# Two of the four sums of the up weights made by adding transfers, values handled in pairs, and eight groups of up tiles by seven products

## The chip, the cores and the metric

One core of one Trainium2 chip runs the whole program in one launch. The metric is the device time of one execution in microseconds (us), the median over several runs. The engines named here are PE (TensorE matmuls; its weight loads are PEld), DVE (VectorE), ACT (ScalarE), POOL (GpSimd), SP (SyncE, which issues most transfers), and 16 DMA engines that move the data.

## The reference, cut to what matters

The block takes 256 tokens, puts 16 learned meta tokens in front, and runs one layer: RMSNorm, one input projection, two kinds of attention (8 heads each), an output projection with residual, then a gated MLP. All data are float32. The change touches the MLP and, in time, what runs beside the attention:

```python
def conv_glu(x, w_gate, w_up, conv_w, conv_b, w_down):   # x (1, 272, 2048); D_FF = 5632
    g = x @ w_gate
    u = x @ w_up
    gp = jnp.pad(g, ((0, 0), (pad, pad), (0, 0)))
    gc = conv_b
    for i in range(CONV_W):                              # CONV_W = 3
        gc = gc + conv_w[i] * gp[:, i:i + L]
    return (jax.nn.silu(gc) * u) @ w_down
```

## The kernel before

Every float32 matmul is made of three matmuls on fp32r halves: a number is split into a rounded part ("hi", by ACT) and a rest ("lo", by DVE), and hi·hi, hi·lo and lo·hi are added in PSUM (`mm3`, lines 606 to 608). So each weight passes ACT once (`whi<-raw`, line 238) and DVE once (`wlo<-raw,whi`, line 242). Weights come in pieces of 128 rows by up to 1024 columns into five buffers `raw` (one more, `more_raw`, in the MLP); the halves have four buffers each (`whi`, `wlo`). A buffer `raw` is free for the next load when the lo split has read it.

The hidden width 5632 is 44 tiles of 128 features. `gate` and `up` are worked in pairs of tiles. Plainly, a pair takes four pieces of 1024 columns, and a piece is eight blocks of three matmuls. Six groups of four up tiles (`QUADS`, the group starts at tile 4, 10, 16, 22, 28, 36) are worked differently: the product of the tokens with four tiles is split in quarters for each pair of 128-row blocks, and seven products of quarters replace eight ("scheme"). For each of the eight row pairs of a group the weights' four quarters come as one piece of 1024 columns (`w_up_s`), and four sums of quarters have to be made from them: `weight_sums` does it with three subtractions on DVE, one 512 columns wide (two sums at once) and two of 256. The seven weight operands (three quarters, four sums) are split like any weights, in two pieces of 768 and 1024 columns. The sums of the tokens' quarters, S, are kept in `near` (a part of the later value buffer) or read again from DRAM (`s_up`). At a group's end `quad_out` combines the seven products on DVE and turns them with eight 128x128 transposes on PE (line 284). `w_down` has the same scheme for half of its columns, with its sums made on DVE as well.

A gate pair goes through `gated` (scale, a three-tap convolution on ACT and DVE, SiLU); `tile_up` or `quad_value` multiplies it with up; `finish_value` splits the value into `act` and, with both tiles of a pair there, `value_sums` forms the sums for `w_down_s` and `save_sums` stores them in DRAM (`s_down`). Tiles on this way sit in twelve buffers `mt` of 258 columns.

The order of everything is set when the program is built. `Flow` runs the generators with a cost for each instruction, and takes whichever can start first; what comes out is one fixed list for each engine. On the chip each engine works its list from the front, and a wait at the front holds all behind it. SP's list holds the loads (`load_weights`, `load_piece`). POOL's list holds, in the attention, the small copies `qs` and `p` (`meta_copies`, made before a softmax row is transposed on PE), the residual sums `res`, and `kr`, the sum of squares (`sum_h`) from which `scale_h` makes the factor `s_2` that the first gate and up tiles wait for. `work` is the list of MLP pieces: around each group's 16 scheme pieces the pieces of gate and up pairs are spread.

## Time and profile before

| what | value |
|---|---|
| median of 3 runs (lowest to highest) | 1108.91 us (1108.28 to 1108.98) |
| the profiled execution: its own time / its span | 1108.62 us / 1106.7 us |
| PE, DVE, ACT, POOL busy | 99%, 90%, 66%, 13% of the span |
| moved by DMA | 239.41 MB, mean 216 GB/s |
| granted TensorE clock | full over the whole span |

The profile was taken from one execution on the chip. Its page and its views give, for stretches or for groups of instructions, the time that an engine was busy, the mean time of one instruction, and what ended an engine's idle time. The roughly 2 us between the span and the execution's time lie outside the program's instructions. In time order PE works on the attention (to about 280 us), the output projection (280 to 376, with the last heads' rest beside it), gate and up with the groups (to 871), and down (to the end).

### The profile page before, as it was taken

The page shows a single profiled execution, that of the slowest core. Times are in us where ns is not written, and L with a number is a line of the kernel's source. Part 1 is how long each engine was busy: PE and PEld are TensorE (multiplying, and loading weights), DVE is VectorE, ACT ScalarE, POOL GpSimd, SP SyncE. Part 2 cuts the span into 40 slices and gives each one's busy share as a digit, 9 for nine tenths or more (in the row PEclk, how much of TensorE's full clock was granted, in tenths as well). Part 3 has the DMA queues.
Part 4 walks back from the last instruction along what each step waited for, and adds up shares of the span by engine and source line. Part 5 has one row for each costly group of instructions (what it writes and reads, how often), then busy time and mean ns, then how long its engine had stood idle before and what let it go on. Part 6 is the DMA issues. An engine that isn't in the chain of part 4 may idle for free.

```text
span 1106.7 us, 22544 instructions
## 1 busy us (share of the span) xinstructions
PE 1100.6 (99%) x8414; PEld 1061.8 (96%) x8414; DVE 990.8 (90%) x1837; ACT 735.1 (66%) x1470; POOL 140.0 (13%) x202
## 2 busy tenths in 40 slices
PE   9999999999999999999999999999999999999998
PEld 9999999999999999999999999999999988888888
DVE  8979888888878989999999999988988999999984
ACT  8788979798647776656666565665565565655663
POOL 3211222121433400000000000000000011100114
PEclk9999999999999999999999999999999999999999
DMA  9553434444665796657667577777688787777772
GB/s 323 199 172 124 148 127 151 139 163 134 230 188 161 207 343 229 198 181 243 224 193 230 179 248 241 238 229 244 203 275 299 260 299 250 251 258 266 281 249 77
DMA packets 72374, 239.41 MB, mean 216 GB/s; under 512 B 8136, under 2 KB 12744, under 8 KB 72264
## 3 DMA queue, kind: packets, MB, share of 16 engines
q1 hardware_dynamic: 71976, 237.69, 63.8%
q8 instruction: 66, 1.08, 0.4%
q14 instruction: 44, 0.36, 0.1%
q10 hardware_dynamic: 288, 0.27, 0.1%
HBM read 219.44 MB, written 17.83 MB: 214 GB/s over the span
## 4 chain that ended last, share of the span: by engine, by line
PE 90%; ACT 4%; DVE 3%; issue 1%; DMA 1%; POOL 0%; DVEq 0%; POOLq 0%; ACTq 0%
PE bank L278 24%; PE bank L606 18%; PE bank L607 18%; PE bank L608 18%; PE bank L1870 6%; PE bank L1871 3%; PE bank L284 2%; ACT whi L238 1%; ACT scr L238 1%; DVE wlo L242 1%; DVE scr L250 1%; DMA raw<-in_w_cq 1%; ACT qraw L238 0%; ACT bank L238 0%; DVE cols L258 0%
## 5 line engine op out<-in xcount | busy, mean ns | idle before, releaser
L238 ACT ACTIVATE whi<-raw 128x512 fp32r<-128x512 f32 (+2 forms) x479 | 358.1, 764 | 173.2 <-PE bank L607 83.5
L242 DVE TENSOR_TENSOR wlo<-raw,whi 128x512 fp32r<-128x512 f32 (+2 forms) x479 | 414.9, 885 | 43.2 <-ACT whi L238 42.1
L606 PE MATMUL bank<-hl,whi 128*128 128x258 f32 (+2 forms) x1528 | 438.5, 287 | 0.1
L607 PE MATMUL bank<-hl,whi 128*128 128x258 f32 (+2 forms) x1528 | 433.7, 284 | 0.0
L608 PE MATMUL bank<-hl,wlo 128*128 128x258 f32 (+2 forms) x1528 | 433.0, 283 | 0.2 <-DVE wlo L242 0.2
L608 PEld LDWEIGHTS bank<-hl,wlo 128*128 128x128 f32 x1528 | 290.1, 190 | 0.9 <-DVE wlo L242 0.7
L607 PEld LDWEIGHTS bank<-hl,whi 128*128 128x128 f32 x1528 | 289.6, 190 | 0.1
L606 PEld LDWEIGHTS bank<-hl,whi 128*128 128x128 f32 x1528 | 288.6, 189 | 0.5 <-ACT scr L238 0.3
L238 ACT ACTIVATE whi<-quarters 128x1024 fp32r<-128x1024 f32 x88 | 81.5, 950 | 64.8 <-PE bank L1870 46.0
L278 PE MATMUL bank<-whi,act 128*128 128x256 f32 (+1 forms) x420 | 111.5, 317 | 0.0
L1870 PE MATMUL bank<-act,whi 128*128 128x512 f32 x308 | 110.1, 397 | 0.0
L242 DVE TENSOR_TENSOR wlo<-quarters,whi 128x1024 fp32r<-128x1024 f32 x88 | 99.4, 1156 | 10.8 <-ACT whi L238 10.2
L266 POOL TENSOR_TENSOR mt<-mt,mt 128x256 f32<-128x256 f32 x7 | 6.8, 979 | 652.4 <-ACT mt L238 652.4
L1871 PE MATMUL bank<-act,wlo 128*128 128x256 f32 x308 | 86.4, 281 | 0.0
L278 PE MATMUL bank<-whi,sin 128*128 128x512 f32 (+1 forms) x272 | 83.5, 355 | 0.0
L278 PEld LDWEIGHTS bank<-whi,act 128*128 128x128 f32 x420 | 74.1, 189 | 5.7
L1870 PEld LDWEIGHTS bank<-act,whi 128*128 128x128 f32 x308 | 57.8, 188 | 13.9
L278 PE MATMUL bank<-whi,hl 128*128 128x256 f32 x288 | 66.5, 280 | 0.0
L278 PE MATMUL bank<-wlo,act 128*128 128x256 f32 (+1 forms) x210 | 66.3, 315 | 0.0
L238 ACT ACTIVATE whi<-more_raw 128x1024 fp32r<-128x1024 f32 (+2 forms) x46 | 44.1, 962 | 24.4 <-PE bank L607 9.9
L1871 PEld LDWEIGHTS bank<-act,wlo 128*128 128x128 f32 x308 | 58.1, 189 | 1.6
L278 PEld LDWEIGHTS bank<-whi,sin 128*128 128x128 f32 x272 | 49.5, 188 | 7.7
(278 smaller groups left out, 1947.9 us busy)
## 6 DMA issues: line engine op xcount, KB each, us to landing
raw<-in_w_gate SPq DMA_DIRECT2D x83, 512.0 KB, 5.0
raw<-in_w_in SPq DMA_DIRECT2D x52, 512.0 KB, 3.9
raw<-in_w_up_s SPq DMA_DIRECT2D x44, 512.0 KB, 4.9
quarters<-in_w_down_s SPq DMA_DIRECT2D x44, 512.0 KB, 6.9
raw<-in_w_up SPq DMA_DIRECT2D x34, 512.0 KB, 5.5
raw<-in_w_out SPq DMA_DIRECT2D x32, 512.0 KB, 4.0
raw<-in_w_down SPq DMA_DIRECT2D x32, 512.0 KB, 5.2
s_down<-sums SPq DMA_DIRECT2D x22, 512.0 KB, 4.1
```

The lines of the kernel that those rows point to most:

```text
L238: nc.scalar.activation(out, in_, f, **kw)
L242: nc.vector.tensor_tensor(out, a, b, op)
L250: nc.vector.scalar_tensor_tensor(out, a, s, b, op0, op1)
L266: nc.gpsimd.tensor_tensor(out, a, b, op)
L278: nc.tensor.matmul(o, l, r, start=start, stop=stop)
L284: nc.tensor.transpose(o, i, ident[:n, :n])
L606: nc.tensor.matmul(ps, whi, xhi, start=start, stop=False)
L607: nc.tensor.matmul(ps, whi, xlo, start=False, stop=False)
L608: nc.tensor.matmul(ps, wlo, xhi, start=False, stop=stop)
L1870: nc.tensor.matmul(ps, whi, x, start=start, stop=False)
L1871: nc.tensor.matmul(ps[:, :n], wlo, x[:, 0, :], start=False, stop=stop)
```

## The change

Four things are changed together.

1. **Sums by transfers.** A new thread `weight_sums_T` (started with the others, running once the tokens' squares are summed, some 34 us into the program) goes over the eight groups and, in steps of two row pairs, issues a transfer from DRAM to DRAM on SP (256 rows of 512 columns, 512 KB, into `t_up`) and, after it has landed, a second one on POOL's queue that adds the neighbouring columns to it (`accum_op=ALU.add`). That gives two of the four sums, with changed signs. 32 copies and 32 adding transfers are issued. In the MLP `load_pair` then loads each row pair's two sums (128x512, 256 KB) into the buffer where DVE used to make them, and `weight_sums` does only the two additions of 256 columns. The signs in `weight_sums`, `value_sums`, `quad_out` and `scheme_out` follow; the down part keeps its three instructions.
2. **Eight groups.** `QUADS` has eight starts in place of six, so eight up tiles that were worked plainly now go through seven products. Around each group stand three pairs of plain gate or up tiles (12 pieces); before there were four or six (16 or 24 pieces). The row pairs of a group are taken in the order `PAIRS`.
3. **Pairs.** Both tiles of a pair share one buffer `two` of 512 columns (four of them; of `mt` two are left). Splits, gate products of a group and value sums run on 512 or 256 columns at once in place of 256 and 128.
4. **Loads of S.** `load_S` for up is issued from `load_piece` two pieces ahead, in a thread of its own.

```diff
-QUADS = (4,10,16,22,28,36)
+QUADS = (4, 8, 14, 18, 24, 28, 34, 38)
+PAIRS = (0, 5, 1, 6, 2, 7, 3, 4)
+AHEAD_S = 2
...
+    TG = 2
+    sums_T = [
+        [(dpool.tile([TG, P, 512], F32, name=f"t_up{w}_{j}"), Event()) for j in range(KC // 2 // TG)]
+        for w in range(len(QUADS))
+    ]
+
+    def weight_sums_T():
+        yield ev_sum_x
+        for w, parts in enumerate(sums_T):
+            for j, (t, ev) in enumerate(parts):
+                src = io["w_up_s"][w][j * TG : (j + 1) * TG]
+                fl.cur.eng = None
+                yield "sp", 0
+                nc.sync.dma_start(t, src[:, :, :512])
+                fl.cur.t += 9000.0
+                yield "pool", 0
+                nc.gpsimd.dma_start(t, src[:, :, 256:768], accum_op=ALU.add)
+                fl.set(ev, 10000.0)
+                fl.cur.t += 2000.0
...
-        g, end = f // 2, (*QUADS, FC)[w + 1] // 2
-        rest = tile_pair("gate", g) + tile_pair("gate", g + 1)
-        for i in range(g + 2, end):
-            rest += tile_pair("gate", i) + tile_pair("up", i)
+        g = f // 2
+        rest = tile_pair(*(("up", g + 2) if w % 2 else ("gate", g + 4)))
+        rest = tile_pair("gate", g) + rest + tile_pair("gate", g + 1)
...
         if r.of == "down":
-            yield from load_S()
+            yield from load_S(r)
+        else:
+            (t, ev), i = r.T
+            yield ev
+            yield "sp", 600
+            load(r.sums[:, : 2 * r.q], t[i], r.ev_T, nc.sync)
...
         if r.of == "down":
             r.sums = yield from one(sums4)
-        t, raw, q = r.sums, r.raw, r.q
-        yield from TT(t[:, : 2 * q], raw[:, q : 3 * q], raw[:, : 2 * q], ALU.subtract)
+            yield from TT(r.sums[:, : 2 * q], r.raw[:, : 2 * q], r.raw[:, q : 3 * q], ALU.add)
+        else:
+            yield r.ev_T
+        t, raw = r.sums, r.raw
         fl.set(r.summed[0])
-        yield from TT(t[:, 2 * q : 3 * q], raw[:, 2 * q : 3 * q], t[:, :q], ALU.subtract)
-        yield from TT(t[:, 3 * q :], t[:, 2 * q : 3 * q], raw[:, 3 * q :], ALU.subtract)
+        yield from TT(t[:, 2 * q : 3 * q], t[:, q : 2 * q], raw[:, :q], ALU.add)
+        yield from TT(t[:, 3 * q :], t[:, 2 * q : 3 * q], raw[:, 3 * q :], ALU.add)
...
-        mts = Slots(tiles(mpool, 12, [P, NT], "mt"))
+        mts = Slots(tiles(mpool, 2, [P, NT], "mt"))
+        twos = Slots(tiles(mpool, 4, [P, 2 * SEQ], "two"))
...
-        yield from TT(A22, A21, A22, ALU.add)
-        yield from TT(A21, A11, A21, ALU.subtract)
-        yield from TT(A11, A22, A11, ALU.subtract)
-        yield from TT(A12, A12, A11, ALU.subtract)
+        yield from TT(b[:, 0:2], repeated(b[:, 1], 2), b[:, 0:4:3], ALU.subtract)
+        yield from TT(b[:, 3], b[:, 0], b[:, 3], ALU.subtract)
+        yield from TT(b[:, 2], b[:, 2], b[:, 3], ALU.add)
...
+    def quad_values(i, pt):
+        for c in range(2):
+            yield ev_gate[2 * i + c]
+        yield from TT(pairs[i], pt, pairs[i], ALU.mult)
+        fl.put(acc, pt)
+        yield from finish_values(i)
...
+    fl.spawn(weight_sums_T(), 3)
```

Three places show how the engines' lists change. First POOL in the attention, at the first pair of heads (`qs` are the gathered query columns, `p` the softmax rows). Before:

```order
L1326 COPY qs_187<-mqr_243 128x2x2 x2
L266 TENSOR_TENSOR p_163<-p_163 128x16
L266 TENSOR_TENSOR p_164<-p_164 128x16
L266 TENSOR_TENSOR p_165<-p_165 128x16
L266 TENSOR_TENSOR p_163<-p_163 128x16 x2
L266 TENSOR_TENSOR p_164<-p_164 4x16
```

and with the change:

```order
L327 DMA t_up_3_85<-in_w_up_s 256x512
L1363 COPY qs_219<-mqr_275 128x2x2 x2
L269 TENSOR_TENSOR p_195<-p_195 128x16
L269 TENSOR_TENSOR p_196<-p_196 128x16
L327 DMA t_up_0_86<-in_w_up_s 256x512
L269 TENSOR_TENSOR p_197<-p_197 128x16
L269 TENSOR_TENSOR p_195<-p_195 128x16 x2
L269 TENSOR_TENSOR p_196<-p_196 4x16
L327 DMA t_up_1_87<-in_w_up_s 256x512
```

Adding transfers now stand between the copies; each waits there for its copy of 512 KB to have landed. Of the 32, 21 stand ahead of the last `p` copy of the attention.

Second POOL at the change from the output projection to the MLP, where `kr` gathers the sum for `s_2`. Before:

```order
L266 TENSOR_TENSOR kr<-kr,scr_157 128x258
L266 TENSOR_TENSOR kr<-kr,scr_158 128x258
L266 TENSOR_TENSOR kr<-kr,scr_159 128x258
L266 TENSOR_TENSOR kr<-kr,scr_162 128x258
L266 TENSOR_TENSOR kr<-kr,scr_160 128x258
L266 TENSOR_TENSOR kr<-kr,scr_161 128x258
```

and with the change:

```order
L327 DMA t_up_3_109<-in_w_up_s 256x512
L269 TENSOR_TENSOR kr<-kr,scr_190 128x258
L269 TENSOR_TENSOR kr<-kr,scr_191 128x258
L269 TENSOR_TENSOR kr<-kr,scr_194 128x258
L269 TENSOR_TENSOR kr<-kr,scr_192 128x258
L327 DMA t_up_0_110<-in_w_up_s 256x512
L269 TENSOR_TENSOR kr<-kr,scr_193 128x258
```

Three adding transfers (one is five rows further up) stand among the fifteen additions, the last of them four additions before the end.

Third DVE in the first group of up tiles (`raw` and `more_raw` hold weights and their sums). Before:

```order
L242 TENSOR_TENSOR more_raw_5379<-raw_82 128x512
L242 TENSOR_TENSOR more_raw_5379<-raw_82,more_raw_5379 128x256
L242 TENSOR_TENSOR more_raw_5379<-more_raw_5379,raw_82 128x256
L242 TENSOR_TENSOR wlo_92<-raw_81,whi_88 128x1024
L242 TENSOR_TENSOR wlo_89<-raw_82,whi_85 128x512
L242 TENSOR_TENSOR wlo_89<-raw_82,whi_85 128x256
L242 TENSOR_TENSOR wlo_90<-raw_84,whi_86 128x1024
```

and with the change:

```order
L245 TENSOR_TENSOR raw_117<-raw_117,more_raw_5454 128x256 x2
L245 TENSOR_TENSOR wlo_125<-raw_115,whi_121 128x1024
L245 TENSOR_TENSOR wlo_126<-raw_118,whi_122 128x1024
L245 TENSOR_TENSOR wlo_123<-more_raw_5454,whi_119 128x512
L245 TENSOR_TENSOR wlo_123<-more_raw_5454,whi_119 128x256
L245 TENSOR_TENSOR wlo_124<-raw_116,whi_120 128x1024
```

The sum of 512 columns is gone from each row pair; the two of 256 and the splits of 512, 256 and 1024 columns stay.

More of the change, by code (lines that the diff above doesn't have):

```diff
@@ L47 @@
 ST = SF // P
[L48 removed]
+QUADS = (4, 8, 14, 18, 24, 28, 34, 38)
+PAIRS = (0, 5, 1, 6, 2, 7, 3, 4)
+AHEAD_S = 2
 def near_to(g):
[L53 removed]
+    return sum(f <= FC - KC + 2 * g for f in QUADS)
 AHEAD, BEHIND = 3, 8
@@ L494, in load_piece @@
         p = pieces[n_loads[0]]
+        for u in pieces[n_loads[0] + AHEAD_S : n_loads[0] + AHEAD_S + 1]:
+            if isinstance(u, Quarters) and u is u.pair.pieces[0] and u.pair.of == "up":
+                fl.spawn(load_S(u.pair))
         n_loads[0] += 1
@@ L502, in load_piece, with load_S @@
         load(p.raw[:, : p.n], p.src, p.loaded, nc.sync)
+    def load_S(r):
+        if r.near:
+            r.ev_S = ev_near[r.g]
+            return
+        r.S = yield from one(s_parts)
+        src, saved = saved_sums[r.of][r.g]
+        yield saved
+        yield "sp", 600
+        load(r.S, src, r.ev_S, nc.sync)
     def load_pair(r):
@@ L635, in hl_free @@
         fl.put(quarters if i < 2 else sums4, t)
-    dpool = ctx.enter_context(tc.tile_pool(name="dpool", bufs=1, space=bass.MemoryType.DRAM))
     saved_sums = {
@@ L1750, in mlp_buffers, with gates @@
             load(near[i], dst, ev_near[i], nc.sync)
-    gates, ev_gate = [None] * FC, [Event() for _ in range(FC)]
-    def gated(f, gate):
+    pairs, ev_gate = [None] * (FC // 2), [Event() for _ in range(FC)]
+    def gates(i, pss):
         yield ev_mlp
-        gs = yield from one(mts)
-        yield from TT(gs[:, : SEQ + 1], gate[:, : SEQ + 1], s_2[:, : SEQ + 1], ALU.mult)
-        fl.put(acc, gate)
-        gc = yield from one(mts)
-        g_ = gc[:, :SEQ]
+        pairs[i] = yield from one(twos)
+        for c, gate in enumerate(pss):
+            gs = yield from one(mts)
+            yield from TT(gs[:, : SEQ + 1], gate[:, : SEQ + 1], s_2[:, : SEQ + 1], ALU.mult)
+            fl.put(acc, gate)
+            fl.spawn(gated(2 * i + c, gs, pairs[i][:, c * SEQ : (c + 1) * SEQ]))
@@ L1786, in finish_value, with finish_values @@
+    def finish_values(i):
+        f, u = 2 * i, pairs[i]
         if f >= FC - KC:
             yield ev_far[(f - FC + KC) // 2]
-        yield from ACT(act[:, f, 0, :], u_, AF.Copy)
-        yield from TT(act[:, f, 1, :], u_, act[:, f, 0, :].bitcast(F32), ALU.subtract)
-        fl.set(ev_act[f])
-        values[f] = u
-        if f ^ 1 in values:
-            yield from value_sums(
-                *saved_sums["down"][f // 2], *(values[i][:, :SEQ] for i in (f & ~1, f | 1))
-            )
-            for i in (f & ~1, f | 1):
-                fl.put(mts, values[i])
@@ L1799, in encoder_block @@
-    values = {}
-    def value_sums(dst, saved, a, b, place=None):
-        (A11, A21), (A12, A22) = ((t[:, :P], t[:, P:SEQ]) for t in (a, b))
-        yield from TT(A22, A21, A22, ALU.add)
-        yield from TT(A21, A11, A21, ALU.subtract)
-        yield from TT(A11, A22, A11, ALU.subtract)
-        yield from TT(A12, A12, A11, ALU.subtract)
+        u_ = u.rearrange("p (f t) -> p f t", f=2)
+        yield from ACT(act[:, f : f + 2, 0, :], u_, AF.Copy)
+        yield from TT(
+            act[:, f : f + 2, 1, :], u_, act[:, f : f + 2, 0, :].bitcast(F32), ALU.subtract
+        )
@@ L1889, in mlp_weights @@
                 if q == 3:
-                    for c in range(2):
-                        fl.spawn((gated if kind == "gate" else tile_up)(2 * which + c, pss[c]))
+                    fl.spawn((gates if kind == "gate" else ups)(which, pss))
                 if kind == "up" and which == FC // 2 - 1:
@@ L1969, in quad_out @@
         U = [[out[:, (2 * i + j) * 2 * P : (2 * i + j + 1) * 2 * P] for j in range(2)] for i in range(2)]
-        m = yield mts, 2
-        c, u3 = (t[:, :SEQ] for t in m)
+        m = yield from one(twos)
+        c, u3 = m[:, :SEQ], m[:, SEQ:]
         yield from ACT(c, P7[1], AF.Copy)
```

118 lines of the change are left out of this document (51 added, 67 removed).

## The prediction

> **What bounds the kernel now.** I read the busy time by stage first, then who PE waited for, then the chain of work that ended last, then single rows. By stage (columns: stretch, its length, then busy us and number of instructions of PE, PEld, DVE, ACT, POOL; then granted clock, DMA share, GB/s):
>
> ```profile
> 60.00:310.00 250.00, 249.14 (x2056) 245.97 (x2055) 219.35 (x570) 210.22 (x646) 58.33 (x111) 1.00 0.47 153
> 310.00:400.00 90.00, 90.00 (x753) 90.00 (x752) 76.71 (x144) 59.02 (x113) 30.23 (x23) 1.00 0.65 208
> 400.00:870.00 470.00, 470.00 (x3937) 470.00 (x3936) 435.39 (x800) 288.55 (x452) 0.00 (x0) 1.00 0.70 232
> 870.00:1050.00 180.00, 180.00 (x908) 151.65 (x907) 171.68 (x185) 104.85 (x125) 19.09 (x15) 1.00 0.76 267
> 1050.00:1107.00 57.00, 52.80 (x319) 46.82 (x317) 38.26 (x42) 28.05 (x39) 15.53 (x14) 1.00 0.47 168
> ```
>
> PE is busy without a gap from 310 to 1050 us, at full clock. In the attention it lacks 0.86 us of 250. DVE has 93% in gate and up, so it is close behind. What PE waited for, in all:
>
> ```profile
> PE bank L278 <- POOL sq8r L266: 0.5, 2, 0.3
> PE bank L608 <- DVE wlo L242: 0.2, 1, 0.2
> ```
>
> So PE bounds every stage but the start and the last 57 us: only fewer or shorter matmuls make it faster, and whatever makes a PE operand late makes it slower at once. The chain around one group of up tiles gives the price of matmuls without their overlap (start, us, what):
>
> ```profile
> 476.60 1.06 PE bank L278 x9
> 480.51 1.43 PE bank L278 x12
> 490.13 0.87 PE bank L284 x8
> ```
>
> A matmul of 256 columns costs 1.43 / 12 = 0.119 us, and in gate and up 470 / 3937 = 0.119 as well. The eight transposes at a group's end cost 0.87 us.
>
> **The change, part by part.** *Eight groups.* Plainly, four up tiles take 4 x 16 x 3 = 192 matmuls. By seven products they take 8 x 7 x 3 = 168, and eight transposes. Per group: 24 x 0.119 = 2.85 us gone, 0.87 us added, so 1.98. Two more groups: **-3.96 us**, on PE, which has no gap there, so it shortens the path one for one if nothing makes PE wait.
>
> *DVE and ACT in gate and up.* The rows that price them:
>
> ```profile
> L242 DVE TENSOR_TENSOR wlo<-raw,whi 128x1024 fp32r<-128x1024 f32 x178 | 218.3, 1232 | 27.9 <-ACT whi L238 27.7
> L242 DVE TENSOR_TENSOR wlo<-raw,whi 128x512 fp32r<-128x512 f32 x255 | 182.6, 728 | 15.3 <-ACT whi L238 14.4
> L242 DVE TENSOR_TENSOR raw<-raw,raw 128x256 f32<-128x256 f32 x50 | 21.1, 422 | 1.2
> L242 DVE TENSOR_TENSOR raw<-raw 128x512 f32<-128x512 f32 x25 | 17.1, 683 | 2.6 <-DMA raw<-in_w_up_s 2.6
> L242 DVE TENSOR_TENSOR mt<-mt,mt 128x128 f32<-128x128 f32 x66 | 17.8, 282 | 0.1
> L238 ACT ACTIVATE sums<-mt 128x256 fp32r<-128x256 f32 x44 | 16.9, 403 | 5.9 <-DMA s_down<-sums 5.2 <-DVE mt L242 0.7
> L238 ACT ACTIVATE whi<-raw 128x512 fp32r<-128x512 f32 x256 | 156.0, 623 | 35.0 <-PE bank L607 25.6 <-DMA raw<-in_w_up_s 5.9 <-PE bank L278 1.6
> ```
>
> The sums by transfers take 6 x 8 = 48 instructions of 512 columns from DVE: 48 x 0.683 = -32.8 us. Two more groups add 16 of 512 and 62 of 256 (splits, the two sums left, the combination): 16 x 0.683 + 62 x 0.422 = +37.1. Pairs trade 106 of 256 and 60 of 128 for 68 of 512: 46.4 - 44.7 - 16.9 = -15.2. DVE: **-10.9 us**. ACT: 68 of 512 for 86 of 256, 42.4 - 34.7 = **+7.7 us**, and it has 180 idle us there. Neither moves the end, since PE is the bound. What must be looked at is the stretch of the scheme's 16 pieces, where fewer plain pieces now stand between. Per row pair DVE takes 0.728 + 0.422 + 1.232 for the splits and 2 x 0.422 for the sums, 3.23 us, against 21 x 0.119 = 2.50 on PE; before, with the 0.683, 3.91. A plain piece is 1.23 on DVE and 24 x 0.119 = 2.86 on PE. Eight pairs and seven plain pieces: 34.4 of 40.0 us. Before, mostly with eleven: 44.8 of 51.5. Room for the values' work is 14% against 13%, and the five plain pieces after it (6.2 of 14.3 us) take the rest. I cost it at nothing; its cover is that 14%, and were it gone the lo halves would be late for PE.
>
> *Loads in the MLP.* 64 loads of 256 KB come new on SP, each issued after the weights of its row pair. Rows of transfers (tile, queue, count, KB each, median us from issue to landing), and the queue's sum (packets, MB, share of 16 engines):
>
> ```profile
> raw<-in_w_in SPq DMA_DIRECT2D x52, 512.0 KB, 3.9
> s_down<-sums SPq DMA_DIRECT2D x22, 512.0 KB, 4.1
> quarters<-in_w_down_s SPq DMA_DIRECT2D x44, 512.0 KB, 6.9
> raw<-in_w_kv_up SPq DMA_DIRECT2D x8, 256.0 KB, 3.6
> ...
> q1 hardware_dynamic: 71976, 237.69, 63.8%
> ```
>
> A MB costs 0.638 x 1106.7 / 237.69 = 2.97 us of all 16 engines, so the 16.8 MB cost 50 us in 470: the share rises from 0.70 to 0.81. One lands in 3.6 us, beside a split queue four pieces (11 us of PE) deep. Nothing on the path.
>
> *The 32 copies and 32 additions beside attention and output projection.* No row shows a transfer from DRAM to DRAM, one that adds, or one issued by POOL. Landing: a copy reads and writes, so from 3.9 us (a load alone) to 8.0 (load and store, 3.9 + 4.1); I take 6. SP's issue of it (first row below: least, median and longest ns of one; median 0.43 us) is hidden: SP sits waiting for free buffers most of the time, though a copy behind such a wait starts late by up to 6.5 us. POOL's issue: from SP's 0.43 to the longest POOL work, 1.54; I take 1.0, midway.
>
> ```profile
> L488 SPq DMA_DIRECT2D s_up<-sums x4: 424/427/985, 353.3 to 387.3; - x4
> SPq L488 <- DVE wlo L242: 436.5, 199, 6.5
> L266 POOL TENSOR_TENSOR kr<-kr,scr 128x258 f32<-128x258 f32 x15 | 23.0, 1536 | 30.9 <-ACT scr L238 30.4
> L266 POOL TENSOR_TENSOR p<-p 128x16 fp32r<-128x16 f32 x40 | 13.1, 330 | 52.9 <-ACT p L238 44.7 <-PE bank L607 3.5 <-PE bank L608 3.5
> 96.92 0.40 POOL L266 TENSOR_TENSOR p<-p 128x16 fp32r<-128x16 f32 x1 [7.16 <-ACT p L238]
> 97.53 0.49 PE L284 MATMUL bank<-ident,p 128*128 128x128 f32 x3
> ```
>
> What is queued behind it on POOL are the forty `p` copies, and PE waits for these: a copy that ends at 97.32 us is followed by its transposes at 97.53, a slack of 0.2 us. POOL is otherwise idle (58 of 250 us busy), so a copy is late only if it comes due while an issue holds POOL. With h us of hold for each of the 21 additions that stand ahead of the last `p` copy: 21h / 250 of forty copies are hit, 3.36h, and each loses h/2 - 0.2. For h = 1: 3.36 x 0.3 = **+1.0 us**. The bounds are 0 (h = 0.43) and 3.36 x 1.54 x 0.57 = 2.9; a gain has no source, since nothing is taken off the attention.
>
> A rule of the Trainium skill speaks against this part: "SBUF — State Buffer", section "SBUF: two separate sides", says that transfers issued by GpSimd have their descriptors written by it, and that it cannot write them while VectorE runs an operation that holds the port pair they share, such as some of its copies. No run here shows it. The nearest candidate in this trace is the scaling of `p`:
>
> ```profile
> L246 DVE TENSOR_SCALAR p<-p,cols 128x272 f32<-128x272 f32 x32 | 11.2, 354 | 1.1
> ```
>
> By that rule each issue could be held by one of these, an estimate of h = 1.35 and +2.2 us in place of +1.0, so 1107.1 in place of 1105.9.
>
> *The change to the MLP.* Three additions are issued among the fifteen `kr` additions. `kr` feeds the ones matmul at 390.31:
>
> ```profile
> 383.62 2.63 POOL L266 TENSOR_TENSOR kr<-kr,scr 128x258 f32<-128x258 f32 x2 [2.43 <-ACT scr L238]
> 387.74 0.41 ACT L238 ACTIVATE parts_sq<-kr 128x258 fp32r<-128x258 f32 x1
> 390.31 0.40 PE L278 MATMUL bank<-parts_sq,ones_r 128*128 128x258 f32 x2
> ```
>
> POOL idled 2.4 us just before its last two, and between its end (386.25) and ACT's read lie 1.5 us: an issue of 1.0 fits. Nothing.
>
> *Sum.* 1108.62 (the profiled execution: span 1106.7, 1.9 around it) - 3.96 + 1.0 = 1105.66. The median of the runs is 0.29 above that execution, so **1105.9 us**, 0.27% below 1108.91. A difference under 0.2%, 2.2 us, can hardly be told from none.
>
> **The rivals.** *POOL held for the copies' landing (slower).* POOL's addition waits at the front of its list for the copy; the list allows 9 us from its issue. Were copies to land later (weights ahead of them on the same queue, SP itself waiting up to 6.5 us), h becomes 1 plus the lateness. The loss is 1.68h² - 0.67h: the gain is gone at h = 1.75, 0.2% slower at h = 2.1, and h = 3 gives +13, so 1118. For it: the 0.2 us of slack, and 21 such waits. Against it: the longest landing median of 512 KB here is about 7, and 8.0 is my upper bound.
>
> *The transfers' bandwidth (no change).* "DMA: Bandwidth & Descriptors", section "Issuing engines are not separate DMA queues", of the Trainium skill says that transfers from all queues share the same 16 engines; no row here has POOL's. By the price above 0.52 MB is 1.56 us of them. About 16 of the 64 transfers fall into 310 to 400, where the share is 0.65: at 1.56 each it is 0.93, at 1.56 for a copy and 3.1 for an addition (two reads) 1.06, an excess of 6 us. The split pieces in front of PE cover 11, but `kr` and the weights come late together, and I give it 2 to 4 us: 1108. From 4.7 for an addition on, the excess passes the cover.
>
> *The values' buffers (slower).* Six buffers in place of twelve hold a pair until its group is done. PE has eight banks, a gate pair waits in two of them. If each of the eight groups makes PE wait 0.9 us, +7 eats the gain twice: 1112. Against it: DVE has less to do, and no wait of PE is seen in 400 to 870 now.
>
> **How the numbers follow.** The forecast (1104.9 to 1106.9, by the bounds 0 and +2.0 of the attention) has 0.58; bandwidth, or the attention's upper bound, 0.20; POOL held 0.16; buffers 0.06. Faster by over 0.2% is the first, within it the second, slower the last two: 0.58, 0.20, 0.22. The range reaches from 1104.4 (half a us below the bound, for the scatter of runs) to 1113, which takes in the bandwidth case, the buffers and the part of the POOL case up to h of about 2.5, and leaves out no more than 2 in 10.
>
> **What would show it.** Right: PE's instructions fall by 32, its busy time by about 4 us, without a gap in gate and up; DVE's busy time falls by some 11 us and the 512-column sums are gone from `raw`; in the attention PE's missing time grows from 0.9 to about 2 us, and POOL's waits name `t_up` seldom. Wrong: waits of `p` or of PE's transposes for transfers or POOL; copies that land later than 9 us; weights that come late between 310 and 400; PE waiting for banks at a group's start.

## The result, and the profile after

The changed kernel took 1117.85 us, the median of 4 runs (1115.11 to 1119.93), against 1108.95 in runs of the kernel before beside it: 0.80% slower, ratio 1.0080 (95% interval 1.0057 to 1.0104). The forecast was 1105.9 with a range up to 1113. The profiled execution took 1119.93 us, the slowest of the four; its span is 1118.2, 11.5 above that of before.

By stage, with the columns and the first four stretches of the prediction (the fifth reaches to the new end):

```profile
60.00:310.00 250.00, 242.38 (x1963) 238.93 (x1962) 211.53 (x554) 205.42 (x634) 71.61 (x127) 0.98 0.84 229
310.00:400.00 90.00, 90.00 (x751) 90.00 (x750) 75.20 (x133) 54.93 (x105) 37.91 (x35) 1.00 0.97 283
400.00:870.00 470.00, 467.53 (x3908) 466.38 (x3907) 430.64 (x740) 300.69 (x446) 1.78 (x2) 1.00 0.80 270
870.00:1050.00 180.00, 180.00 (x941) 152.85 (x940) 171.65 (x193) 105.81 (x125) 20.15 (x15) 1.00 0.76 270
1050.00:1119.00 69.00, 63.96 (x375) 56.22 (x373) 49.37 (x53) 34.60 (x45) 15.56 (x14) 0.98 0.51 177
```

In the attention (first row) PE lacks 7.6 us of 250, before 0.9; the granted clock is 0.98, before 1.00; the share of the DMA engines is 0.84, before 0.47. From 400 to 870 it lacks 2.5 us, before nothing. What PE, then DVE, then POOL waited for:

```profile
PE bank L281 <- DVE sq8r L257: 5.5, 3, 2.3
PE bank L281 <- POOL sq8r L269: 1.9, 5, 0.5
PE bank L281 <- DVE wlo L245: 1.5, 2, 1.0
DVE scr L245 <- DMA scr<-scr: 9.2, 4, 3.6
POOL t_up L327 <- DMA t_up<-in_w_up_s: 50.1, 11, 11.9
```

PE itself never waits for `p` nor for a transfer (one of its weight loads waits 0.3 us for `p`). It waits for `sq8r`, a cast on DVE, and DVE waits for `scr<-scr`: four transfers of 32 KB that swap the halves of the rotary parts of two heads (`rope`, issued by SP). Before, this wait was one of 1.2 us:

```profile
DVE scr L242 <- DMA scr<-scr: 1.2, 1, 1.2
```

Transfers of before (first row) and after (the others; the last column is the median from issue to landing), and the two queues:

```profile
scr<-scr SPq DMA_DIRECT2D x16, 32.2 KB, 2.3
```

```profile
scr<-scr SPq DMA_DIRECT2D x16, 32.2 KB, 6.0
raw<-in_w_in SPq DMA_DIRECT2D x52, 512.0 KB, 5.4
t_up<-in_w_up_s SPq DMA_DIRECT2D x32, 512.0 KB, 8.3
t_up<-in_w_up_s POOLq DMA_DIRECT2D x32, 512.0 KB, 8.7
q1 hardware_dynamic: 89320, 269.16, 70.4%
q0 software_dynamic: 8704, 16.78, 9.4%
```

The swaps land in 6.0 us (median) instead of 2.3. One of the two worst places, row by row (SP, then DVE, then PE; in brackets the idle time before the row and what ended it):

```profile
172.99 1.80 SPq L516 DMA_DIRECT2D scr<-scr  x3
174.84 0.59 SPq L324 DMA_DIRECT2D t_up<-in_w_up_s  x1
175.47 0.60 SPq L516 DMA_DIRECT2D scr<-scr  x1
...
183.33 0.43 DVE L245 TENSOR_TENSOR scr<-scr,consts 128x258 f32<-128x258 f32 x1 [2.23 <-DMA scr<-scr]
183.67 0.16 DVE L257 CAST sq8r<-sq 128x8 fp32r<-128x8 f32 x1
183.74 0.68 DVE L245 TENSOR_TENSOR wlo<-raw,whi 128x512 fp32r<-128x512 f32 x1
184.34 0.44 DVE L253 SCALAR_TENSOR_TENSOR scr<-scr,scr 128x272 f32<-128x272 f32 x1
...
183.89 0.17 PE L281 MATMUL bank<-ones_r,sq8r 128*4 128x2 f32 x1 [1.79 <-DVE sq8r L257]
184.54 0.22 PE L281 MATMUL bank<-ones_r,sq8r 128*4 128x2 f32 x3 [0.49 <-POOL sq8r L269]
```

The product with the swapped halves stands at the front of DVE's list and waits for the last swap; behind it stands the small cast that PE needs. 2.28 us of PE are gone, and then its clock goes down (stretches of 1 us; the clock is the third column from the end):

```profile
183.00:184.00 1.00, 0.11 (x1) 0.08 (x1) 0.67 (x3) 0.31 (x1) 0.09 (x1) 1.00 1.02 379
185.00:186.00 1.00, 1.00 (x6) 1.00 (x6) 1.00 (x4) 0.58 (x2) 1.00 (x2) 0.50 0.21 84
187.00:188.00 1.00, 1.00 (x7) 1.00 (x7) 1.00 (x4) 1.00 (x4) 0.00 (x0) 0.50 0.78 115
188.00:189.00 1.00, 1.00 (x8) 1.00 (x8) 0.62 (x3) 0.92 (x3) 0.00 (x0) 0.83 0.83 186
```

PE counts as busy there, but its matmuls begin 0.22 us apart instead of 0.12, so 6 or 7 of them touch a stretch of 1 us instead of 10 or 11. The same happens at 246 us. The bill against the span of before: -4.0 for the two groups, +6.8 of PE idle in the attention, +4.7 of clock (the stretches 180:190, 240:250 and 250:260 have 0.83, 0.82 and 0.84, which makes 5.1; some 0.4 of it fell on idle time of PE at 246.4 to 247.4 that is counted already), +2.5 between 400 and 870: 10.0 of 11.5 us; 1.5 is not placed. The mean clock of this execution is 0.995, that of the three others 0.997 to 0.998, so the clock took about half as much of them.

### The profile page after: what moved, and what is told of

It reads as the page before. It is cut to its first block, busy times and chain, and to the rows that moved or that the text cites. A ratio compares the mean times of both kernels' runs of the same rounds, so it can differ in the third digit from the quotient of the medians.

```text
span 1118.2 us, 22654 instructions
## 1 busy us (share of the span) xinstructions
PE 1102.5 (99%) x8382; PEld 1061.9 (95%) x8382; DVE 987.5 (88%) x1769; ACT 746.4 (67%) x1452; POOL 165.6 (15%) x234
## 3 DMA queue, kind: packets, MB, share of 16 engines
q0 software_dynamic: 8704, 16.78, 9.4%
## 4 chain that ended last, share of the span: by engine, by line
PE 81%; DVE 6%; ACT 5%; DMA 5%; issue 2%; POOL 0%; SPq 0%; DVEq 0%; ACTq 0%; POOLq 0%
PE bank L281 25%; PE bank L644 15%; PE bank L645 15%; PE bank L646 15%; PE bank L1907 6%; PE bank L1908 3%; DVE wlo L245 3%; ACT whi L241 2%; PE bank L287 2%; DMA raw<-in_w_gate 2%; DMA raw<-in_w_up 1%; ACT scr L241 1%; DMA raw<-in_w_cq 1%; DVE scr L253 1%; DMA raw<-in_w_q_up 1%
## 5 line engine op out<-in xcount | busy, mean ns | idle before, releaser
L245 DVE TENSOR_TENSOR wlo<-raw,whi 128x512 fp32r<-128x512 f32 (+2 forms) x498 | 436.6, 892 | 38.3 <-ACT whi L241 34.6
L644 PE MATMUL bank<-hl,whi 128*128 128x258 f32 (+2 forms) x1400 | 404.4, 289 | 0.0
L646 PE MATMUL bank<-hl,wlo 128*128 128x258 f32 (+2 forms) x1400 | 399.4, 285 | 1.1 <-DVE wlo L245 0.9
L645 PE MATMUL bank<-hl,whi 128*128 128x258 f32 (+2 forms) x1400 | 399.3, 285 | 0.0
L646 PEld LDWEIGHTS bank<-hl,wlo 128*128 128x128 f32 x1400 | 267.7, 191 | 2.0 <-DVE wlo L245 1.9
L645 PEld LDWEIGHTS bank<-hl,whi 128*128 128x128 f32 x1400 | 267.6, 191 | 0.1
L644 PEld LDWEIGHTS bank<-hl,whi 128*128 128x128 f32 x1400 | 266.7, 191 | 0.1
L281 PE MATMUL bank<-whi,act 128*128 128x256 f32 (+1 forms) x580 | 146.6, 307 | 0.0
L281 PEld LDWEIGHTS bank<-whi,act 128*128 128x128 f32 x580 | 101.6, 189 | 5.8
L281 PE MATMUL bank<-wlo,act 128*128 128x256 f32 (+1 forms) x290 | 89.3, 308 | 1.0 <-DVE wlo L245 1.0
L281 PE MATMUL bank<-whi,hl 128*128 128x256 f32 x384 | 88.7, 280 | 0.0
L281 PEld LDWEIGHTS bank<-whi,hl 128*128 128x128 f32 x384 | 68.4, 190 | 0.0
L281 PEld LDWEIGHTS bank<-wlo,act 128*128 128x128 f32 x290 | 54.8, 189 | 4.2 <-DVE wlo L245 1.2
```

The source lines that it names most:

```text
L245: nc.vector.tensor_tensor(out, a, b, op)
L281: nc.tensor.matmul(o, l, r, start=start, stop=stop)
L644: nc.tensor.matmul(ps, whi, xhi, start=start, stop=False)
L645: nc.tensor.matmul(ps, whi, xlo, start=False, stop=False)
L646: nc.tensor.matmul(ps, wlo, xhi, start=False, stop=stop)
```

## The experiments

In the table "lost" is what PE lacks of 250 us between 60 and 310 us; share and swaps (median landing of 16) are of the same stretch. These three columns come from one execution of each kernel, the profiled one.

| run | us (median) | ratio to before, 95% interval | share | swaps, us | lost, us |
|---|---|---|---|---|---|
| before | 1108.6 to 1109.0 | | 0.47 | 2.3 | 0.9 |
| no_T_load | 1106.56 | 0.9979 (0.9968 to 0.9989) | 0.47 | 2.5 | 0.9 |
| no_transfers | 1107.25 | 0.9986 (0.9977 to 0.9995) | 0.47 | 2.3 | 0.9 |
| copies_only | 1107.62 | 0.9988 (0.9978 to 0.9997) | 0.61 | 2.2 | 0.9 |
| pool_only | 1107.94 | 0.9992 (0.9983 to 1.0001) | 0.61 | 3.8 | 0.8 |
| half_odd | 1113.95 | 1.0055 (1.0038 to 1.0072) | 0.68 | 5.1 | 2.1 |
| paced18 | 1119.45 | 1.0096 (1.0081 to 1.0111) | 0.72 | 5.9 | 2.1 |
| adds_repeat | 1112.66 | 1.0037 (1.0025 to 1.0050) | 0.75 | 6.0 | 3.5 |
| copies_triple | 1113.62 | 1.0042 (1.0025 to 1.0059) | 0.87 | 4.9 | 3.5 |
| plain_double | 1123.04 | 1.0137 (1.0106 to 1.0169) | 0.86 | 5.8 | 5.8 |
| rope_later | 1116.45 | 1.0070 (1.0055 to 1.0085) | 0.86 | 6.3 | 5.7 |
| pipelined | 1118.67 | 1.0093 (1.0066 to 1.0120) | 0.84 | 5.3 | 6.1 |
| after | 1117.85 | 1.0080 (1.0057 to 1.0104) | 0.84 | 6.0 | 7.6 |
| swap_act | 1121.77 | 1.0115 (1.0100 to 1.0130) | 0.85 | 5.5 | 7.9 |
| hold_only | 1143.15 | 1.0308 (1.0288 to 1.0327) | 0.55 | 4.2 | 22.1 |
| six_dve | 1111.03 | 1.0017 (1.0007 to 1.0026) | 0.47 | 2.4 | 0.8 |
| seven_dve | 1120.27 | 1.0106 (1.0089 to 1.0123) | 0.47 | 2.2 | 0.9 |
| dve_sums | 1121.02 | 1.0111 (1.0093 to 1.0129) | 0.47 | 2.6 | 0.8 |
| pool_sums | 1142.63 | 1.0302 (1.0286 to 1.0318) | 0.47 | 2.4 | 0.9 |
| accum_mlp | 1227.78 | 1.1067 (1.1027 to 1.1107) | 0.47 | 2.4 | 0.8 |

**First question: which transfers cost?** My first theory was the place: a copy stands between the third and the fourth swap in SP's list.

`no_transfers`:

```diff
-            yield ev
...
-            load(r.sums[:, : 2 * r.q], t[i], r.ev_T, nc.sync)
+            load(r.sums[:, : 2 * r.q], r.src[:, : 2 * r.q], r.ev_T, nc.sync)
...
-    fl.spawn(weight_sums_T(), 3)
```

> The changed kernel without the 32 copies and 32 additions; the two sums are read from the weights themselves (so the up values are wrong), all else stays, the 64 loads in the MLP too. Theory 1 (the transfers beside the attention make it slow, above all where a rotary swap on SP's queue lands late, DVE waits for it at the front of its list, and the cast that PE needs stands behind): the PE gaps at about 75, 184 and 246 us are gone and so is the lower clock behind two of them; 1105 to 1106. Rival (the MLP part, that is pairs, fewer buffers, eight groups, is what costs): 1109 or more, with PE gaps in 400 to 870.

`copies_only`:

```diff
-                yield "pool", 0
-                nc.gpsimd.dma_start(t, src[:, :, 256:768], accum_op=ALU.add)
```

> The 32 copies stay on SP, the 32 additions on POOL are left out (so two sums are wrong). Theory 1 with the copy as the culprit (it stands on SP's queue between or ahead of the four swaps of a rotary key): DVE still waits for the swaps, gaps at 184 and 246 us stay, 1111 to 1117. Rival (POOL's issue or wait, or the additions' use of the engines): 1105 to 1107.

`pool_only`:

```diff
-                nc.sync.dma_start(t, src[:, :, :512])
...
-                nc.gpsimd.dma_start(t, src[:, :, 256:768], accum_op=ALU.add)
+                nc.gpsimd.dma_start(t, src[:, :, 256:768])
```

> The 32 copies on SP are left out; POOL issues 32 plain transfers of the same 512 KB without waiting for anything (two sums wrong). Theory 1 with the copy as the culprit: hardly a wait for the swaps, 1105 to 1108; what is over 1105 is the price of POOL's 0.9 us of issue, forecast as 1.0 in all. Rival (POOL's issue holds the p copies back): 1110 or more.

`rope_later` (the planner is told that the swap lands 5 us later, so it puts the product behind the cast):

```diff
             load(tmp[i * half : ...], t[j * half : ...], swapped, nc.sync)
+            swapped.time += 5000.0
```

> The whole changed kernel, but the order's cost for the rotary swaps is 5 us longer, so DVE's product with the swapped rows stands 8 to 17 instructions further back, behind the cast that PE waits for; all transfers stay. Theory 1: the gaps at 75, 184 and 246 us and the lower clock behind them are gone, 11 us of them; what is left is the late loads at 400 to 460 (2 us): 1106 to 1109. Rival (transfers' bandwidth or POOL held for the copies' landing): at most 2 us better than 1117.9.

Without transfers 1107.25, with the copies 1107.62, with POOL's plain transfers 1107.94: each kind alone is free, and PE's loss in the attention is that of before. The first two are above what I had expected (1105 to 1106 and 1105 to 1107); the fourth question goes into that. The copies alone land in 5.7 us, near my 6, and stand among the swaps just the same: at 172.25 us in `copies_only` a copy is issued ahead of three of the four swaps, and the swaps land in 2.2 us. So the place theory fell. `rope_later` was a miss (1106 to 1109 expected): it kept the clock at 1.00 and took away the waits for `sq8r`, but PE lost 5.7 us in other places and the kernel took only 1.4 less than the change (the intervals overlap). The swap is one victim of several.

**Second question: is it POOL, held at the front of its list, or the load?** In the changed kernel POOL sits 26.4 us before an addition ahead of 300 us.

`pipelined` (copy n, then addition n-1; `every` is the list of all 32 steps):

```diff
...
+        for n in range(len(every) + 1):
+            if n < len(every):
+                t, ev, src = every[n]
...
+                nc.sync.dma_start(t, src[:, :, :512])
+            fl.cur.t += 9000.0
+            if n > 0:
+                t, ev, src = every[n - 1]
...
                 nc.gpsimd.dma_start(t, src[:, :, 256:768], accum_op=ALU.add)
```

> The same 32 copies and 32 additions at the same pace, but each addition is issued one step later, behind the next copy, some 20 us after its own copy instead of 9: POOL finds the copy landed and is not held. If the holding of POOL's list costs the time, this runs in 1106.5 to 1108.5 us, as the runs with only copies or only plain transfers do, and POOL's waits for the tiles (50.1 us in the changed kernel) go to under 10. If the joint load of copies and read-and-write additions makes all small transfers late, the load is the same, the share of the DMA engines stays at 0.8 to 0.9 between 50 and 300 us, the rotary swaps stay late, and it takes 1113 us or more.

`adds_repeat` (`parts_T` are the first group's four tiles):

```diff
-                nc.sync.dma_start(t, src[:, :, :512])
+                t = parts_T[j][0]
+                if w == 0:
+                    nc.sync.dma_start(t, src[:, :, :512])
```

> Only the first four copies; all 32 additions go into those four tiles again and again (two of the up weights' four sums are then wrong). This is the additions' load alone: their reading and writing of the engines, 9.4% of them, without the copies' 28 transfers and almost without a wait of POOL. If the holding of POOL costs the time, or only the joint load does: 1107 to 1108.5 us. If the additions themselves slow the small transfers of the attention: 1112 us or more, with rotary swaps that land in 7 us and waits of TensorE for sq8r at 50 to 250 us.

`paced18`:

```diff
-                fl.cur.t += 9000.0
+                fl.cur.t += 16000.0
```

> The planned gap from a copy to its addition goes from 9 to 16 us, the period from 11 to 18: the same transfers are spread from 50 to some 630 us instead of 50 to 410. POOL is held less often and the joint load falls by a third in the attention (share 0.65 to 0.75). By either theory it is nearer to the runs without additions: 1107 to 1110 us. If it stays above 1113, a single collision of one copy, one addition and one swap is enough, and neither the holds nor the mean load count.

`hold_only`:

```diff
-                nc.sync.dma_start(t, src[:, :, :512])
...
-                nc.gpsimd.dma_start(t, src[:, :, 256:768], accum_op=ALU.add)
+                nc.gpsimd.dma_start(t, src[:, :, 256:768])
+                nc.gpsimd.dma_start(spare[w][j], t[1, 127:, 448:])
```

> No copies and no additions: POOL issues a plain transfer of 512 KB per step, and right behind it a transfer of 256 bytes that reads its last row, so that POOL is held at the front of its list until the first has landed, some 5 us in each of 32 steps (two of the up weights' four sums are then wrong). The load of the engines is that of the run with plain transfers alone (1107.9 us). If the holding of POOL is what costs the time, it shows here more than in the changed kernel, whose holds before 300 us are some 30 us in all: 1113 us or more, with waits of TensorE for sq8r and of VectorE for the swap at 170 to 260 us. If the load costs it: 1107 to 1109 us.

`plain_double`:

```diff
-                nc.gpsimd.dma_start(t, src[:, :, 256:768], accum_op=ALU.add)
+                nc.gpsimd.dma_start(spare[2 * w][j], src[:, :, 256:768])
+                nc.gpsimd.dma_start(spare[2 * w + 1][j], src[:, :, 512:])
```

> The 32 copies stay; in place of each addition POOL issues two plain transfers of 512 KB into spare tiles (two of the up weights' four sums are then wrong). Software transfers take about the additions' share of the engines (2 times 4.7%, against 9.4%) with no addition in them. If the sum of the load costs the time, whatever kind it is: 1113 us or more and a share of 0.8 to 0.9 between 50 and 300 us. If it is something of the additions (that they follow each other, their reading and writing at the target): 1107 to 1110 us.

`pipelined` cut POOL's holds ahead of 300 us from 26.4 to 9.5 us and gained nothing. Over the runs holds and cost do not go together: `swap_act` has 9.9 us of holds there and costs 13.0 us against before, `rope_later` 21.3 and 7.7. What still held POOL in `pipelined` is a finding of its own. POOL's rows at two additions, the idle time before the second of each pair, and the landing of the first:

```profile
162.03 0.91 POOL L333 DMA_DIRECT2D t_up<-in_w_up_s  x1
173.09 0.91 POOL L333 DMA_DIRECT2D t_up<-in_w_up_s  x1 [4.85 <-issue]
...
224.69 0.89 POOL L333 DMA_DIRECT2D t_up<-in_w_up_s  x1
234.71 0.92 POOL L333 DMA_DIRECT2D t_up<-in_w_up_s  x1 [3.54 <-issue]
```

The additions of 162.03 and 224.69 landed after 10.7 and 9.7 us, at 172.7 and 234.4, and the next were issued 0.3 to 0.4 us later, though their copies had long landed. No addition of the changed kernel, of this one or of `adds_repeat` starts sooner than 0.25 us after the one before has landed, and three, seven and six of them within half a us of that. But being an addition is not enough to wait: in `accum_mlp`, whose additions are half as large and go to SBUF (on-chip memory) instead of DRAM, 17 of them are issued before the one before has landed. And plain transfers wait too, the fourth for the first: in `plain_double` POOL issues at 43.65, 44.36 and 44.91 us, then not until 51.61, when the first has just landed (51.2), and never has more than three on the way. By the packets of the queue's rows an addition of 512 KB has 8704 / 32 = 272, one of 256 KB and a plain transfer of 512 KB have 144. So a limit on what POOL's queue has on the way, somewhere between 3 x 144 = 432 and 2 x 272 = 544 packets, would fit all of these; that is an inference, no run varied it.

`adds_repeat`, almost without copies, costs 5.4 us against `no_transfers`: the additions slow the small transfers by themselves (6.0 us at a share of 0.75). Copies at 0.61 did not (2.2), and POOL's plain transfers at 0.61 did less (3.8) and at no cost.

`hold_only` says what a held POOL looks like. It cost 34.6 us (150 us of holds in all), and by another way than the change (PE's waits, then POOL's):

```profile
PE bank L287 <- POOL p L269: 25.7, 8, 5.3
POOL spare L332 <- DMA t_up<-in_w_up_s: 150.1, 29, 8.1
```

The softmax's transposes wait for `p`. PE has no such row in the changed kernel. So the rival mechanism exists, and is not what happened. My expectation named the wrong victim (`sq8r`).

`plain_double` has no addition, POOL waits for no copy in it, the share is about the same, and the loss is greater: 1123.04. So it takes no addition. It isn't load alone yet, for POOL still issues, and stands idle before some of its issues ahead of 300 us, held by its own queue:

```profile
POOL spare L334 <- issue: 9.0, 3, 6.1
```

`copies_triple` below takes POOL out. In `paced18` the transfers go on to 640 us and hit the feed-forward part instead: PE busy and DMA share in two stretches there, and what DVE waited for:

```profile
500.00:550.00 50.00, 47.19 (x384) 45.73 (x383) 41.66 (x74) 27.78 (x41) 2.68 (x3) 1.00 0.94 297
550.00:600.00 50.00, 48.02 (x398) 47.48 (x397) 43.80 (x72) 31.06 (x46) 1.79 (x2) 1.00 0.91 303
```

```profile
DVE raw L245 <- DMA raw<-t_up: 15.0, 9, 3.5
```

That was a miss: I had expected 1107 to 1110. Less load here is more load there.

**Third question: SP's queue, POOL, or the 16 engines?**

`copies_triple`:

```diff
-                fl.cur.t += 9000.0
-                yield "pool", 0
-                nc.gpsimd.dma_start(t, src[:, :, 256:768], accum_op=ALU.add)
+                fl.cur.t += 5000.0
+                yield "sp", 0
+                nc.sync.dma_start(spare[2 * w][j], src[:, :, 256:768])
+                yield "sp", 0
+                nc.sync.dma_start(spare[2 * w + 1][j], src[:, :, 512:])
...
-                fl.cur.t += 2000.0
+                fl.cur.t += 6000.0
```

> POOL issues nothing: SP issues the copy and, 5 us later, two more plain transfers of 512 KB into spare tiles per step (two of the up weights' four sums are then wrong). The bytes are those of the run with plain transfers in pairs on POOL (1123.0 us). If it is the load of the DMA engines, whoever issues it: 1113 us or more, late rotary swaps, and share 0.8 to 0.9 between 50 and 300 us. If POOL's issuing (29 to 36 us in all) or its queue had the blame there: 1107 to 1109 us.

`swap_act`:

```diff
-            yield "sp", 600
+            yield "act", 60
...
-            load(tmp[i * half : ...], t[j * half : ...], swapped, nc.sync)
+            load(tmp[i * half : ...], t[j * half : ...], swapped, nc.scalar)
```

> The changed kernel, with the rotary swaps (32 transfers of 32 KB) issued by ACT instead of SP, on ACT's queue, which carries nothing else in the attention; ACT has room of 5 to 10 us in 50 there. If the swaps are late because they stand behind transfers of 512 KB in SP's queue, they land in 3 us or less and the gaps at 184 and 246 us and the half clock behind them go: 1108 to 1112 us. If they are late because the 16 engines that both queues share are busy, they land in 5 us or more again: 1115 us or more.

The swaps' rows of `copies_only`, `copies_triple` and `swap_act`:

```profile
scr<-scr SPq DMA_DIRECT2D x16, 32.2 KB, 2.2
```

```profile
scr<-scr SPq DMA_DIRECT2D x16, 32.2 KB, 4.9
```

```profile
scr<-scr ACTq DMA_DIRECT2D x16, 32.2 KB, 5.5
```

On a queue of their own the swaps land hardly sooner (5.5 us against 6.0) and the kernel is no faster: it isn't SP's queue, which leaves the 16 engines behind all queues. The Trainium skill states in "DMA: Bandwidth & Descriptors", section "Issuing engines are not separate DMA queues", that transfers from all of them run on the same 16 engines; this trace agrees. And with POOL out of it altogether, three plain transfers per step on SP make the swaps late and cost 4.8 us against before, 6.4 against `no_transfers`, with 3.5 us of PE's time lost in the attention. That is the part shown to be load alone. The changed kernel loses 7.6 us there at no higher share; what makes the rest, the software queue's part (POOL's issues, the holds, the additions' own way of moving), is not separated. That what POOL's queue carries weighs more than its share is seen twice: the swaps of `adds_repeat` are later at 0.75 than those of `copies_triple` at 0.87 (6.0 and 4.9 us), and those of `pool_only` later than those of `copies_only` at the same 0.61 (3.8 and 2.2).

**Fourth question: where did the 3.96 us go even without transfers, and was there a cheaper way?**

`no_T_load`, `dve_sums` and `pool_sums` drop the thread and the loads of sums, and make the two sums (in the first: a copy in their place) by one line each; the name behind it is the run's:

```diff
+            yield from ACT(r.sums[:, : 2 * q], r.raw[:, : 2 * q], AF.Copy)                            # no_T_load
+            yield from TT(r.sums[:, : 2 * q], r.raw[:, : 2 * q], r.raw[:, q : 3 * q], ALU.add)        # dve_sums
+            yield from PTT(r.sums[:, : 2 * q], r.raw[:, : 2 * q], r.raw[:, q : 3 * q], ALU.add)       # pool_sums
```

> No transfers, and no loads of the two sums either: ACT copies two of the weights' parts in their place (two sums wrong). In the run without transfers, whose loads of the sums stayed, TensorE lost 1.8 us at 850 to 900 and 0.5 us before it, and 1.5 us of the 3.96 were gained. If those 64 loads of 256 KB cost that (share of the DMA engines near 1.0 at 840 to 875): 1104.5 to 1105.5 us. If the end of the eighth group costs it by its order (VectorE late for the first weights of the down projection): 1106.5 to 1107.5 us, with the same loss at 850 to 900.

> No transfers at all: the pairs of values and the eight groups by seven products stay, and all four sums of the up weights are made on VectorE, as before. VectorE then has about 11 us of work more than the changed kernel over 600 us. If VectorE has room, this gives the gain of the products alone, 1105 to 1107.5 us; if VectorE comes late for the weights (TensorE's waits for wlo and the sums at 500 to 900 us), 1108 us or more.

> No transfers: the two sums that they made are made on POOL, which has nothing to do between 450 and 850 us (64 additions of 128x512, each about 2 us by the 1.0 to 1.25 us that 128x258 takes). If the loads of sums and the transfers were all that cost, and POOL does not slow VectorE: 1104.5 to 1106.5 us, faster than both. If POOL's work slows VectorE's beside it, VectorE comes late for the weights: 1110 us or more.

`half_odd`:

```diff
-        for w, parts in enumerate(sums_T):
+        for w, parts in list(enumerate(sums_T))[1::2]:
...
-                fl.cur.t += 2000.0
+                fl.cur.t += 13000.0
...
-            r.T = sums_T[w][i // TG], i % TG
+            r.T = (sums_T[w][i // TG], i % TG) if w % 2 else None
```

Where `r.T` is None, VectorE makes all four sums.

> Only the odd four of the eight groups get their two sums by copies and additions (16 of each, one pair in 22 us instead of 11); the other four make them on VectorE. The load in the attention is about that of the copies alone (share 0.55 to 0.70), which cost nothing; VectorE's work in the feed-forward part is half way between the changed kernel and the run with all sums on VectorE. If the load sets the cost: 1106 to 1110 us. If each addition costs by itself, half of the changed kernel's loss stays: 1112 to 1115 us.

`accum_mlp`:

```diff
-            (t, ev), i = r.T
-            yield ev
-            yield "sp", 600
-            load(r.sums[:, : 2 * r.q], t[i], r.ev_T, nc.sync)
+            fl.spawn(accumulate(r), 0)
...
+        yield from ACT(r.sums[:, : 2 * r.q], r.raw[:, : 2 * r.q], AF.Copy)
+        yield "pool", 0
+        nc.gpsimd.dma_start(r.sums[:, : 2 * r.q], r.src[:, r.q : 3 * r.q], accum_op=ALU.add)
```

> Nothing is copied or added in DRAM: in the feed-forward part, where POOL is idle, ACT copies two parts of the loaded weights into the sums' tile and POOL adds the other two by 64 transfers of 256 KB from the weights into that tile. The attention is as in the kernel before. The loads of sums fall away, and the additions take about 106 us of the 16 engines over some 450 us (estimate by half of what an addition of 512 KB takes, 3.3 us of 16 engines). If the load is what counts and it stays under 0.9 there: 1104.5 to 1107 us, faster than both. If the additions come late for the weights (each waits for the one before to land, 5 us or more): 1112 us or more, with TensorE's waits for wlo from 430 us on.

`six_dve` and `seven_dve` are `dve_sums` with `QUADS = (4, 10, 16, 22, 28, 36)` and `(4, 10, 16, 22, 28, 34, 38)` and the work list of before:

> One part of the change alone: the values in pairs and the new signs of the sums, with the six groups of the kernel before, all four sums on VectorE and no transfers. TensorE has the kernel before's work, and VectorE less of it. If the values in pairs cost nothing: 1108.0 to 1109.3 us, no change, and VectorE's busy time under the 991 us of before. If they make anything late (their ACT work, the fewer and larger buffers): 1110 us or more.

> The same with seven groups, one more than before: 1.98 us less on TensorE. VectorE's work lies between six groups and the eight that cost 1121.0 us with all sums on VectorE. If VectorE keeps up with seven: 1106.5 to 1107.5 us, faster than both kernels without a single transfer. If it doesn't, TensorE waits for wlo from 500 us on and the gain is gone: 1109 to 1115 us.

`no_T_load` is the groups' worth without any cost of transfers: 2.2 us, not 3.96. The start of the down projection in the kernel before, then in `no_T_load`, and PE's waits there in `no_T_load`:

```profile
850.00:905.00 55.00, 55.00 (x353) 49.82 (x352) 53.16 (x85) 32.80 (x49) 3.43 (x3) 1.00 0.78 276
```

```profile
850.00:905.00 55.00, 53.21 (x327) 46.72 (x326) 51.87 (x72) 31.52 (x40) 3.87 (x3) 1.00 0.79 281
```

```profile
PE bank L1903 <- DVE wlo L245: 1.3, 2, 0.8
PE bank L281 <- DVE wlo L245: 0.5, 1, 0.5
```

1.8 us are given back there: PE reaches the down projection sooner, DVE still has the last group behind it, and its `wlo` are late. 2.2 + 1.8 = 4.0. It stays with the loads of sums and without them, so they are not its cause; between 400 and 850 PE loses nothing.

With all sums on VectorE eight groups cost 1121.02, seven 1120.27 (above both ranges that I had given), and even six, the number of before, 1111.03. PE waits for `wlo` from 500 us on, in `six_dve`:

```profile
PE bank L640 <- DVE wlo L245: 2.1, 3, 0.8
```

though VectorE is busy 986.6 us in all against 990.8 before. So the pairs alone cost 0.17% as long as the two sums stay on VectorE; whether by their longer instructions or by the order `PAIRS`, I didn't separate. POOL cannot take the sums: VectorE's own instructions beside it grow. From 450 to 850 us, of `dve_sums` and of `pool_sums` (count, busy, mean ns):

```profile
L245 DVE TENSOR_TENSOR wlo<-raw,whi 128x1024 fp32r<-128x1024 f32 x121 | 145.3, 1217 | 3.7 <-ACT whi L241 3.5
L245 DVE TENSOR_TENSOR wlo<-raw,whi 128x256 fp32r<-128x256 f32 x45 | 18.8, 417 | 0.0
```

```profile
L245 DVE TENSOR_TENSOR wlo<-raw,whi 128x1024 fp32r<-128x1024 f32 x116 | 152.6, 1329 | 5.1 <-ACT whi L241 5.1
L245 DVE TENSOR_TENSOR wlo<-raw,whi 128x256 fp32r<-128x256 f32 x43 | 23.4, 545 | 0.0
```

The Trainium skill says in "SBUF — State Buffer", section "Who interferes with whom", that a VectorE instruction with two SBUF inputs contends with a GpSimd instruction that reads SBUF; these traces agree, 9% on the long ones and 31% on the short. `accum_mlp`, the largest miss: PE waits 51.6 us for `whi` of ACT and 21.2 for `wlo` there, and the clock falls to between 0.86 and 0.98 in twelve stretches of 50 us; what in the lists made ACT so late I didn't follow up. `half_odd` lost in both places, 1.3 us more than before in the attention and 3.5 between 550 and 850. No version that makes all four sums beat the kernel before.

## Why the prediction was wrong, by its steps

*The eight groups, -3.96 us.* Right as a term: 32 PE instructions fewer (8414 to 8382), and in `no_T_load` PE's busy time is 3.8 us lower. Wrong as a result: "it shortens the path one for one if nothing makes PE wait". At the end of the eighth group something does, for 1.8 us. I looked at the stretch inside a group, not at what stands behind the last one.

*DVE -10.9 us at no cost.* It measured -3.3 (990.8 to 987.5). I multiplied durations, but rows of DVE overlap: the 128x512 split above begins at 183.74 and lasts 0.68, the next row starts at 184.34. So 0.08 us of each duration count twice, and the change has 68 DVE instructions fewer: 5.4 us that were never there. The other 2 are not placed. The cover held with the two sums off VectorE; `dve_sums` (7.9 us of PE's waits for `wlo`) shows it gone with them on it. ACT's +7.7 measured +11.3 (735.1 to 746.4) and moved nothing either.

*Loads in the MLP: nothing.* Share 0.80 (forecast 0.81) and 0.7 us between `no_transfers` and `no_T_load`, inside their intervals.

*The copies' landing.* Alone 5.7 us (forecast 6); beside the additions 8.3, above my upper bound of 8.0. A sum of two landings on a half idle machine is no bound for a busy one.

*POOL's issue, h = 1.0.* Right: 0.90 us in the median, 1.03 at most, and PE never waited for `p`. The rule of the Trainium skill on VectorE's port ("SBUF — State Buffer", section "SBUF: two separate sides"), h = 1.35, isn't seen in the issues: none of the 32 took that long. A delay behind the issue would not show in this number.

***The copies and additions beside the attention, +1.0 us (bounds 0 and 2.9): the step that failed.*** It measured +6.8 us of idle PE and +4.7 of clock. The term priced only what the transfers do to POOL. It took their effect on the other transfers as nothing, and never named the swaps, which land on DVE's path with little to spare. The rows were there: 0.47 of the engines, and by my own price of 2.97 us per MB each pair adds 1.56 for a copy and 3.1 for an addition every 11 us, 0.42 more, 0.89 in all. It measured 0.84.

*The rivals.* "The transfers' bandwidth" had the right mechanism in the wrong place: I counted 310 to 400 alone, where PE in fact lost nothing; weights came late just behind it (a gate piece in 12.8 us at 419) for 2.0 us between 400 and 500, which is near the 2 to 4 I gave it; that the place was another makes this partly luck. Its greater part was in the attention. Its limit was miscounted besides: by the same sum the cover of 11 us is passed at 3.75 us for an addition, not at 4.7; it measured 0.094 x 1118.2 / 32 = 3.3. "POOL held" is real (`hold_only`) but didn't decide here (`pipelined`; and `copies_triple` is slower than before without any hold). "The values' buffers" weren't seen: PE never waited for a bank.

## What to carry to other kernels

When a change adds transfers beside a stage that isn't bound by them, add up the share of the DMA engines over the whole stage, and look for small transfers whose landing is followed at once by an instruction at the front of a list: here swaps of 32 KB went from 2.3 us at a share of 0.47 to between 4.9 and 6.3 from 0.68 on. An engine off the bound that waits for such a transfer holds everything behind it, also the small cast that the bound engine needs. A gain at the end of a stage counts only if the next stage's first operands come earlier too.

## What the hardware showed that I had not expected

- The granted clock fell to 0.50 for 3.4 us at 184.93 us, where PE had been idle for 2.28 us out of 2.4, and for 6.8 us at 246.37, in a wait of 2.8 us, but not around 76 us, where PE was idle for 1.7 us. In steps of 0.05 us the changes of this trace lie at 184.93, 188.34, 246.37 and 253.19: 1, 17 and 2 times 3.41 us apart. In the 3.41 us ahead of the two drops PE was busy for 33% and 44%; the wait at 76 us falls on two such stretches, with 67% and 83%. In `accum_mlp`, cut the same way, PE was busy for 0 to 57% ahead of each of 19 drops, and the least busy stretch without a drop had 46%. This fits a limit near one half on PE's share of fixed stretches better than a limit on the length of a gap. The Trainium skill, "TensorE: Matmul & The Clock Gate", section "Part 1: The HAM clock gate (the "warmup" mystery)", gives one idle window of about 3.4 us that runs freely; the window's length and its running freely agree, but here a window that was half idle was enough.
- POOL's queue holds its engine: the next addition of 512 KB is issued 0.25 us or more after the one before has landed, and a fourth plain transfer of 512 KB after the first of three has.
- An addition of 512 KB takes twice the engines' time of a plain transfer of the same bytes: 32 of them 9.4% of the span on the software queue, 32 plain ones (`pool_only`) 4.7%. POOL's issue of one takes 0.90 us, of a plain one 0.56.
- POOL's additions of 128x512 make VectorE's two-input instructions 9 to 31% longer.
